# Encoder kernel: x and memory also laid out by features, first feed-forward group by blocks of features, x added afterwards

## The chip, the core and the metric

The kernel runs on one core of a Trainium2 chip. The core has TensorE (PE in the profile: matmuls, and PEld: weight loads), VectorE (DVE), ScalarE (ACT), GpSimd (POOL) and SyncE (SP), and 16 DMA engines that all of them start transfers on. SP and ACT start plain transfers; POOL starts those that add to what lies at the destination. The metric is the time of one execution on the device in microseconds, as the median of several runs.

## The reference

Two layers of an encoder over 512 tokens of 1,024 features, all in float32:

```python
for i in range(DEPTH):                     # DEPTH = 2
    y = swiglu(x, ffn_w_gate[i, 0], ffn_w_up[i, 0], ffn_w_down[i, 0])
    x = layer_norm(ALPHA * x + 0.5 * y, ln_g[i, 0], ln_b[i, 0])
    y = mixer_ab(...) if i % 2 == 0 else mixer_c(...)
    x = layer_norm(ALPHA * x + y, ln_g[i, 1], ln_b[i, 1])
    y = memory_attn(x, mem, mem_w_q[i], mem_w_kv[i], mem_w_o[i])
    x = layer_norm(ALPHA * x + y, ln_g[i, 2], ln_b[i, 2])
    y = swiglu(x, ffn_w_gate[i, 1], ffn_w_up[i, 1], ffn_w_down[i, 1])
    x = layer_norm(ALPHA * x + 0.5 * y, ln_g[i, 3], ln_b[i, 3])

def swiglu(x, w_gate, w_up, w_down):       # d_ff = 2816
    return (jax.nn.silu(x @ w_gate) * (x @ w_up)) @ w_down
```

`memory_attn` attends from 512 tokens to 256 memory tokens, whose keys and values are projections of `mem` (256 x 1,024). The mixers attend among the 512 tokens.

## The kernel before

**Numbers in two parts.** Every float32 operand of a product is split into a high part (a cast to float32r on ACT) and a remainder (a subtraction on DVE): `split` at L296. A product is then three matmuls, high x high, high x remainder, remainder x high: `mm3` at L307.

**Where things lie.** The residual x stands in four tiles of 128 tokens x 1,024 features (`self.x`). For products that contract over features, x also stands transposed in `self.xh` and `self.xl` (128 features x 8 blocks x 512 tokens). `to_features` (L384) makes them: four 128x128 transposes on PE into a PSUM bank, then a split out of it.

**A feed-forward step** (`ffn`, L608) goes over five groups of 2 x 256 hidden columns and a rest. For each group it computes the hidden activations of the two column blocks c1 and c2 (`hidden`, L502: 96 matmuls of 512 columns each), then `down_fast` (L518) multiplies them with the down weights by seven block products (Strassen-Winograd), whose sums of weights come partly from accumulating DMAs of POOL, partly from DVE mixes. Its products m are added to halves of the x tiles by DVE when they leave PSUM (`into`, L574); products 1 and 6 go to a separate tile u2. Product 1 of the first group is written by ACT instead (L590). `rest` runs products 7 and 4.

**The opening.** For the first group's c1 (`ffn_by_tokens`, L473), the tokens are the stationary side: for each of four token blocks 2 x 8 x 3 matmuls of 256 columns, so the first block can start once 128 tokens are there. In the very first step (`first`) it also loads x (`load_x`, L1230: 128 rows of 4 KB per tile, in the order of the grid's columns), transposes it, and loads the first weights in between. The gated activations are turned round at the end by eight transposes.

**Memory** (`memory_tokens`, L1137) is called once inside each mixer: it loads `mem` by tokens, transposes it in 16 pieces on PE and splits it.

**Tiles and order.** Tiles come from pools with a fixed number of buffers: 27 "slab" (4 KB per partition), 2 "raw" (8 KB, landing place of weights), 14 "t2" (2 KB), and PSUM banks 3 "a", 2 "d", 3 "t". Operations are recorded in program order (`Graph.record`, L131) and emitted (`emit`, L168) in the order that a list scheduler works out from guessed costs; every engine and DMA queue then runs its own list in order. Buffers of a pool are granted first come, first served in program order. `nc.after` adds an ordering for that planner alone: with it `masks` (two constant tiles) is placed behind the last DMA recorded so far. Because all operations are recorded by helpers, they all carry the line L143 in the profile, and tiles tell them apart: "a", "d" and "t" are PSUM banks (or the t2 tiles, which also show as "t"), "ident" is the identity matrix of the transposes.

Of the kernel before, what the change touches and what calls it, by code (L numbers as in the profile page):

```python
# [24 lines left out]
KB = D // P  # L25
DFF = 2816
MEM = 256
GRID_W = 64
ROWS = S // GRID_W
# [223 lines left out]
class Kernel:  # L253
# [56 lines left out]
        mm(ps, st[0], mv[1], start=False, stop=False, **kw)  # L310
        mm(ps, st[1], mv[0], start=False, stop=last, **kw)

    def weights(self, srcs, shape, pieces, between=None):

        nc = self.nc
        raw = self.tile(self.raw, [P, *shape], F32, "raw")
        for part, src in srcs:
            nc.sync.dma_start(out=part(raw), in_=src)
            if between:
                between()  # L320
                between = None
        got = []
        for piece in pieces:
            v = piece(raw)
            shp = list(v.shape)
            wh, wl = self.slab(F32R, shp), self.slab(F32R, shp)
            self.split(v, wh, wl)
            got.append((wh, wl))
        return got
# [5 lines left out]
            [(lambda r: r, src)], (KB, 256), [lambda r, i=i: r[:, :, i * P : (i + 1) * P] for i in range(2)]  # L335
        )

    def w_cols_k(self, w, c0, between=None):

        src = w[:, c0 : c0 + 256].rearrange("(k p) f -> p k f", p=P)  # L340
        half = [lambda r, i=i: r[:, 4 * i : 4 * i + 4, :] for i in range(2)]
        return self.weights([(half[i], half[i](src)) for i in range(2)], (KB, 256), half, between)

    def w_cols512(self, w, c0):

# [124 lines left out]
            nc.vector.tensor_tensor(out=dst, in0=halves(pu), in1=halves(sg), op=ALU.mult)  # L470
        return sg

    def ffn_by_tokens(self, wg, wu, first, dst):  # L473

        between = None
        if first:
            self.load_x(0, 0, 512)
            self.to_features(0, [0])
            self.nc.after = self.nc.ops[-1], {"scalar", "vector"}
            between = lambda: (self.load_x(0, 512, D), self.to_features(0, [1]))  # L480
        gate, up = self.w_cols_k(wg, 0, between), self.w_cols_k(wu, 0)
        if first:
            self.nc.after = None
            for t in range(1, NT):
                self.load_x(t)
        sgs = []
        for t in range(NT):
            if first and t > 0:
                self.to_features(t)
            both = []  # L490
            for w, tag in ((gate, "a"), (up, "d")):
                ps = self.ps(tag)
                for k in range(KB):
                    mv = [z[:, k % 4, :] for z in w[k // 4]]
                    self.mm3(ps[:, :256], self.xT(k, t * P, (t + 1) * P), mv, k == 0, k == KB - 1)
                both.append(ps[:, :256])
            sgs.append(self.gated(*both, 256))
        for b in range(2):
            ps = self.transposed([(t * P, P, sgs[t][:, b * P : (b + 1) * P]) for t in range(NT)])
            self.nc.scalar.copy(dst[:, :, b, :], ps.rearrange("p (s n) -> p s n", s=2))  # L500
# [14 lines left out]
        self.split(z, hi, lo, scale)  # L515
        return hi, lo

    def down_fast(self, h1, h2, w, r1, r2, coef, u2, last):  # L518

# [3 lines left out]
        nc = self.nc  # L523
# [54 lines left out]
        banks = {}  # L578

        def run(*steps, blocks=range(2)):  # L580
            for m, tag in steps:
                for b in blocks:
                    ps = banks[m, b] = self.ps(tag) if isinstance(tag, str) else banks[tag, b]
                    for q in range(2):
                        st = [z[:, q * 256 + b * P : q * 256 + (b + 1) * P] for z in left[m]]
                        self.mm3(
                            ps, st, [z[:, q] for z in right[m]], isinstance(tag, str) and q == 0, q == 1, skip_group_check=True
                        )
                    v = into[m](b)
                    if m == 1 and first:  # L590
                        nc.scalar.activation(v, ps, AF.Copy, scale=coef)
                    else:
                        c = -coef if m in (5, 7, 3) else coef
                        nc.vector.scalar_tensor_tensor(out=v, in0=ps, scalar=c, in1=v, op0=ALU.mult, op1=ALU.add)

        def gather(*places):
            for t, n in places if last else ():
                op = ALU.add if n is n1 else ALU.subtract
                nc.gpsimd.tensor_tensor(out=x[t][:, n], in0=x[t][:, n], in1=u2[:, t % 2], op=op)

        run((1, "d"), (6, "t"))
        gather((0, n2), (1, n2), (2, n1), (3, n1))
        run((2, 1), (5, "t"))
        gather((2, n2), (3, n2))
        run((3, 5))
        return u2, lambda *blocks: run((7, "d"), (4, 7), blocks=blocks)

    def ffn(self, i, ln_i, last, aside=None):  # L608

        nc = self.nc  # L610
        wg, wu, wd = (self.a[n][i] for n in ("ffn_w_gate", "ffn_w_up", "ffn_w_down"))
        coef, u2 = 0.5 / ALPHA, None
        for g, (c1, c2) in enumerate(((0, 1024), (256, 1280), (512, 1536), (768, 1792), (2048, 2304))):
            h1, h2 = (self.slab(F32, (P, 2, 2, 256)) for _ in range(2))
            if g == 0:
                self.ffn_by_tokens(wg, wu, i == 0, h1)
            else:
                self.hidden(wg, wu, c1, h1)
            self.hidden(wg, wu, c2, h2)
            u2, rest = self.down_fast(h1, h2, wd, c1, c2, coef, u2, g == 4)  # L620
            if g < 4:
                rest(0, 1)
            if g == 0 and aside:
                nc.after = [op for op in nc.ops if op.dma][-1], {"sync"}
                aside()
# [510 lines left out]

    def memory_tokens(self):  # L1137

        raw = self.tile(self.raw, [P, 2, D], F32, "raw")
        self.nc.sync.dma_start(out=raw, in_=self.a["mem"].rearrange("(m p) d -> p m d", p=P))  # L1140
        self.mt = []
        for kk in range(4):
            ps = self.transposed(
                [(j * 256 + m * P, P, raw[:, m, (2 * kk + j) * P : (2 * kk + j + 1) * P]) for j in range(2) for m in range(2)]
            )
            self.mt.append(self.split_t2(ps))

    def memory(self, i, ln_i, last):
        nc, a = self.nc, self.a
# [77 lines left out]
        gb = self.load_ln(ln_i)  # L1227
        self.down(acts[4:], self.w_rows(w_o, 512) + self.w_rows(w_o, 768), 1.0 / ALPHA, {"gb": gb, "last": last})

    def load_x(self, t, lo=0, hi=D):  # L1230
        src = self.a["x"].rearrange("(r c) d -> c r d", c=GRID_W)[16 * t : 16 * t + 16, :, lo:hi]
        self.nc.sync.dma_start(out=self.x[t][:, lo:hi], in_=src)

    def masks(self):
        self.band = self.tile(self.cst, [P, 384], F32, "band")
# [63 lines left out]
def _layout(inputs):  # L1299
    v = {k: np.ascontiguousarray(np.asarray(z)) for k, z in inputs.items()}  # L1300
    rpb = np.pad(v["c_rpb"][0], ((0, 0), (0, 0), (BIAS_L, BIAS_R)))
    a = {
        "x": v["x"].reshape(S, D),
        "mem": v["mem"].reshape(MEM, D),
        "ln_g": v["ln_g"].reshape(8, D),
        "ln_b": v["ln_b"].reshape(8, D),
        "ffn_w_gate": v["ffn_w_gate"].reshape(4, D, DFF),
        "ffn_w_up": v["ffn_w_up"].reshape(4, D, DFF),
        "ffn_w_down": v["ffn_w_down"].reshape(4, DFF, D),
        "ab_w_in": v["ab_w_in"][0],  # L1310
        "ab_w_out": v["ab_w_out"][0],
        "ab_q_gain": v["ab_q_gain"],
        "ab_k_gain": v["ab_k_gain"],
        "ab_sink": v["ab_sink"],
        "c_w_in": v["c_w_in"][0],
        "c_w_out": v["c_w_out"][0],
        "rpb_g": np.stack([rpb[:, 7 - i : 15 - i, :].transpose(0, 2, 1) for i in range(ROWS)], axis=1),
        "mem_w_q": v["mem_w_q"],
        "mem_w_kv": v["mem_w_kv"],
        "mem_w_o": v["mem_w_o"],  # L1320
    }
    a.update(_constants())
    return {k: np.ascontiguousarray(z) for k, z in a.items()}
# [14 lines left out]
```

## Time and profile before

| | us |
|---|---|
| median of 3 runs | 2215.97 (2215.14 to 2216.75) |
| span of the profiled execution, first to last instruction | 2218.7 |
| PE busy in it | 2185.8 |
| DVE busy | 1415.7 |
| ACT busy | 878.2 |
| POOL busy | 318.0 |

Of the profiled execution only the span is known. It is about 0.1% above the median of the runs.

The profile is of one execution. A timeline row reads: start, duration, engine, line, operation, output tile <- input tiles, shape, count, and in brackets the idle time of the engine before it and what ended that. A row of a table of stretches reads: the stretch and its length, then for PE, PEld, DVE, ACT and POOL the busy time and (x) the instructions, then the granted TensorE clock, the busy share of the DMA engines and the GB/s that they moved. A row of the chain in order of time reads: start, duration, what the chain ran through. A matmul row's duration includes the time in the pipeline, so the pace of matmuls is read from the distance of their starts.

### The profile page before, as it was taken

Reading aid. Unit: us, or ns where it says so; the run is one execution under the profiler, and the core shown is the slowest. Engines: PE = TensorE matmul, PEld = TensorE weight load, DVE = VectorE, ACT = ScalarE, POOL = GpSimd, SP = SyncE. Lnnn points to the kernel's source line nnn. Section 1 sums busy time; section 2 is a strip of 40 time slices with the busy share of each in tenths; the row PEclk is TensorE's granted clock in tenths of the full one; section 3 lists DMA queues with packets and bytes.
Section 4 is the critical chain, followed back from the end, with each engine's and each line's share of the span. In section 5 each row is a group of like instructions: output and inputs, shape, how many; then the busy total and the mean of one; then the engine's idle time right before and its main releaser. Section 6 shows DMA issues by size and latency. Waiting matters only on the chain.

```text
span 2218.7 us, 28479 instructions
## 1 busy us (share of the span) xinstructions
PE 2185.8 (99%) x11264; PEld 1863.8 (84%) x11264; DVE 1415.7 (64%) x2127; ACT 878.2 (40%) x1412; POOL 318.0 (14%) x431
## 2 busy tenths in 40 slices
PE   8999999999999999999999999999999999999998
PEld 7888888778998988888888888888989989888886
DVE  5566657788745756655765566567767557566556
ACT  4333333466443433333333233245554434333331
POOL 0000022544000000000300001214330000000002
PEclk9999999999999999999999999999999999999999
DMA  7443333102442642334334444235553325433342
GB/s 222 143 142 120 106 107 104 39 10 70 130 133 96 182 135 95 95 121 149 120 105 131 143 142 147 95 102 148 141 157 124 124 96 161 124 100 93 111 152 67
DMA packets 195221, 265.15 MB, mean 120 GB/s; under 512 B 8848, under 2 KB 139536, under 8 KB 195088
## 3 DMA queue, kind: packets, MB, share of 16 engines
q1 hardware_dynamic: 181136, 231.88, 32.9%
q0 software_dynamic: 13952, 31.46, 6.6%
q8 instruction: 88, 1.44, 0.3%
q14 instruction: 45, 0.37, 0.1%
HBM read 248.63 MB, written 4.19 MB: 114 GB/s over the span
## 4 chain that ended last, share of the span: by engine, by line
PE 94%; DVE 3%; ACT 1%; POOL 1%; DMA 1%; issue 1%; SPq 0%; DVEq 0%; POOLq 0%; ACTq 0%
PE a L143 59%; PE d L143 21%; PE t L143 14%; DVE slab L143 1%; DVE t L143 1%; ACT slab L143 1%; DVE x L143 0%; POOL slab L143 0%; DMA raw<-ab_w_out 0%; ACT t L143 0%; DMA slab<-t 0%; POOL rms8y L143 0%; ACT junk L143 0%; DMA x<-x 0%; POOL lny L143 0%
## 5 line engine op out<-in xcount | busy, mean ns | idle before, releaser
L143 PE MATMUL a<-xh,slab 128*128 128x512 f32 (+1 forms) x2960 | 892.9, 382 | 0.0
L143 PEld LDWEIGHTS a<-xh,slab 128*128 128x128 f32 x2960 | 549.1, 188 | 106.8
L143 PE MATMUL a<-xl,slab 128*128 128x512 f32 (+1 forms) x1480 | 565.1, 382 | 0.0
L143 PE MATMUL d<-slab,slab 128*128 128x512 f32 (+2 forms) x1856 | 448.8, 381 | 3.3 <-ACT slab L143 3.3
L143 DVE TENSOR_TENSOR slab<-raw,slab 128x1024 fp32r<-128x1024 f32 x300 | 368.8, 1250 | 92.7 <-ACT slab L143 92.2
L143 PEld LDWEIGHTS d<-slab,slab 128*128 128x128 f32 x1856 | 334.5, 188 | 67.3 <-ACT slab L143 5.1
L143 ACT CAST slab<-raw 128x1024 fp32r<-128x1024 f32 x300 | 304.3, 1048 | 206.2 <-DMA raw<-ffn_w_gate 176.4
L143 DVE TENSOR_TENSOR slab<-slab,slab 128x1024 fp32r<-128x1024 f32 (+2 forms) x220 | 254.0, 1177 | 177.8 <-ACT slab L143 104.7
L143 PEld LDWEIGHTS a<-xl,slab 128*128 128x128 f32 x1480 | 278.3, 188 | 53.4
L143 PE MATMUL a<-slab,slab 128*128 128x256 f32 (+3 forms) x1720 | 301.2, 321 | 3.7 <-DMA slab<-t 1.4
L143 PEld LDWEIGHTS a<-slab,slab 128*128 128x128 f32 x1720 | 250.0, 190 | 31.4 <-DVE slab L143 4.6
L143 ACT ACTIVATE t<-a 128x512 f32<-128x512 f32 (+3 forms) x105 | 58.1, 554 | 525.7 <-PE a L143 525.6
L143 ACT CAST slab<-slab 128x1024 fp32r<-128x1024 f32 (+1 forms) x180 | 174.3, 1000 | 135.6 <-DVE slab L143 135.5
L143 POOL DMA_DIRECT2D slab<-ffn_w_down x40 | 48.6, 1255 | 1008.7 <-DMA slab<-ffn_w_down 639.6
L143 PE MATMUL t<-slab,slab 128*128 128x512 f32 (+1 forms) x792 | 185.4, 380 | 0.0
L143 PEld LDWEIGHTS t<-slab,slab 128*128 128x128 f32 x792 | 142.9, 188 | 29.8
L143 DVE TENSOR_TENSOR slab<-a,t 128x512 f32<-128x512 f32 x72 | 49.8, 692 | 175.7 <-PE a L143 175.7
L143 DVE TENSOR_TENSOR slab<-t,slab 128x512 fp32r<-128x512 f32 (+2 forms) x213 | 133.1, 649 | 40.0 <-ACT slab L143 39.5
L143 ACT CAST slab<-t 128x512 fp32r<-128x512 f32 (+2 forms) x213 | 114.6, 565 | 100.9 <-PE t L143 61.8
L143 DVE SCALAR_TENSOR_TENSOR x<-d,x 128x512 f32<-128x512 f32 x168 | 114.9, 686 | 47.4 <-PE d L143 46.9
L143 POOL TENSOR_TENSOR t<-t,l 128x256 f32<-128x256 f32 (+2 forms) x104 | 84.2, 831 | 344.1 <-DVE l L143 343.8
L143 PE MATMUL a<-slab,xh 128*128 128x256 f32 (+1 forms) x432 | 101.2, 328 | 2.2 <-ACT slab L143 1.6
(104 smaller groups left out, 1912.5 us busy)
## 6 DMA issues: line engine op xcount, KB each, us to landing
slab<-ffn_w_down SPq DMA_DIRECT2D x100, 512.0 KB
raw<-ffn_w_gate SPq DMA_DIRECT2D x40, 1024.0 KB
raw<-ffn_w_up SPq DMA_DIRECT2D x40, 1024.0 KB
slab<-ffn_w_down POOLq DMA_DIRECT2D x40, 512.0 KB, 9.7
slab<-t SPq DMA_DIRECT2D x96, 128.0 KB
raw<-mem_w_kv SPq DMA_DIRECT2D x8, 1024.0 KB
raw<-mem_w_kv SPq DMA_DIRECT2D x16, 512.0 KB
raw<-mem_w_q SPq DMA_DIRECT2D x8, 1024.0 KB
```

The costliest lines, as they stand in the source:

```text
L143: op.call = lambda: fn(*args, **kw)
```

## The change

The host also passes `x_t` (features x tokens, the tokens in the grid's column order) and `mem_t` (features x memory tokens). The first group of the first feed-forward step computes its c1 by blocks of features (`ffn_by_features`): after a memset and eight matmuls on zeros (`warm`), it loads x and the gate and up weights in five steps of 1, 1, 2, 2 and 2 feature blocks, splits them, and adds each block's products to four PSUM banks, with the weights as the stationary side and 512 tokens as columns. The first step's two weight loads are issued by ACT, all others by SP. The x tiles are no longer loaded at the start: in the first group the products that would be added to them are written by ACT (`fresh`), and after the group x is added to the four tiles by accumulating DMAs of POOL (`add_x`). Memory is loaded by features and split from where it lands.

```diff
+    def warm(self, n):
+
+        nc = self.nc
+        zero = self.junk[:, :512]
+        nc.vector.memset(zero, 0.0)
+        ps = self.ps("t")
+        for i in range(n):
+            nc.tensor.matmul(ps, zero[:, :P], zero, start=i == 0, stop=i == n - 1)
+
+    def ffn_by_features(self, wg, wu, dst):
+
+        nc = self.nc
+        self.warm(8)
+        steps = [(0, 1), (1, 2), (2, 4), (4, 6), (6, 8)]
+        xT = self.a["x_t"].rearrange("(k p) n -> p k n", p=P)
+        raws = [[self.slab(F32, (P, 4, 256)) for _ in range(2)] for _ in range(2)]
+        got = [[[self.slab(F32R, (P, 4, 256)) for _ in range(2)] for _ in range(2)] for _ in range(2)]
+        banks = [[self.ps(tag) for _ in range(2)] for tag in "ad"]
+        for lo, hi in steps:
+            xs = self.slab(F32, (P, 2, 512))
+            n = hi - lo
+            nc.sync.dma_start(out=xs[:, :n], in_=xT[:, lo:hi, :])
+            q, at = lo // 4, slice(lo % 4, lo % 4 + n)
+            for raw, w in zip(raws, (wg, wu)):
+                src = w[:, 0:256].rearrange("(k p) f -> p k f", p=P)
+                (nc.sync if lo else nc.scalar).dma_start(out=raw[q][:, at, :], in_=src[:, lo:hi, :])
+            self.split(xs[:, :n], self.xh[:, lo:hi, :], self.xl[:, lo:hi, :])
+            for raw, parts in zip(raws, got):
+                self.split(raw[q][:, at, :], parts[q][0][:, at, :], parts[q][1][:, at, :])
+            for k in range(lo, hi):
+                for parts, pair in zip(got, banks):
+                    for b, ps in enumerate(pair):
+                        st = [z[:, k % 4, b * P : (b + 1) * P] for z in parts[k // 4]]
+                        self.mm3(ps, st, self.xT(k, 0, S), k == 0, k == KB - 1)
+        for b in range(2):
+            self.gated(banks[0][b], banks[1][b], dst=dst[:, :, b, :])
...
-    def down_fast(self, h1, h2, w, r1, r2, coef, u2, last):
+    def down_fast(self, h1, h2, w, r1, r2, coef, u2, last, fresh=False):
...
-                    if m == 1 and first:
-                        nc.scalar.activation(v, ps, AF.Copy, scale=coef)
+                    c = -coef if m in (5, 7, 3) else coef
+                    if m == 1 and first or m in (2, 5, 3, 4) and fresh:
+                        nc.scalar.activation(v, ps, AF.Copy, scale=c)
                     else:
-                        c = -coef if m in (5, 7, 3) else coef
                         nc.vector.scalar_tensor_tensor(out=v, in0=ps, scalar=c, in1=v, op0=ALU.mult, op1=ALU.add)
...
-            if g == 0:
-                self.ffn_by_tokens(wg, wu, i == 0, h1)
+            if g == 0 and i == 0:
+                self.ffn_by_features(wg, wu, h1)
+            elif g == 0:
+                self.ffn_by_tokens(wg, wu, h1)
             else:
                 self.hidden(wg, wu, c1, h1)
             self.hidden(wg, wu, c2, h2)
-            u2, rest = self.down_fast(h1, h2, wd, c1, c2, coef, u2, g == 4)
+            u2, rest = self.down_fast(h1, h2, wd, c1, c2, coef, u2, g == 4, i == 0 and g == 0)
             if g < 4:
                 rest(0, 1)
+            if g == 0 and i == 0:
+                for t in range(NT):
+                    self.add_x(t)
...
-        raw = self.tile(self.raw, [P, 2, D], F32, "raw")
-        self.nc.sync.dma_start(out=raw, in_=self.a["mem"].rearrange("(m p) d -> p m d", p=P))
+        raw = self.tile(self.raw, [P, KB, MEM], F32, "raw")
+        self.nc.sync.dma_start(out=raw, in_=self.a["mem_t"].rearrange("(k p) m -> p k m", p=P))
         self.mt = []
         for kk in range(4):
-            ps = self.transposed(
-                [(j * 256 + m * P, P, raw[:, m, (2 * kk + j) * P : (2 * kk + j + 1) * P]) for j in range(2) for m in range(2)]
-            )
-            self.mt.append(self.split_t2(ps))
+            self.mt.append(self.split_pair(raw[:, 2 * kk : 2 * kk + 2, :].rearrange("p k m -> p (k m)")))
...
-    def load_x(self, t, lo=0, hi=D):
-        src = self.a["x"].rearrange("(r c) d -> c r d", c=GRID_W)[16 * t : 16 * t + 16, :, lo:hi]
-        self.nc.sync.dma_start(out=self.x[t][:, lo:hi], in_=src)
+    def add_x(self, t):
+        src = self.a["x"].rearrange("(r c) d -> c r d", c=GRID_W)[16 * t : 16 * t + 16]
+        self.nc.gpsimd.dma_start(out=self.x[t], in_=src, accum_op=ALU.add)
...
-        "mem": v["mem"].reshape(MEM, D),
+        "x_t": v["x"].reshape(ROWS, GRID_W, D).transpose(2, 1, 0).reshape(D, S),
+        "mem_t": v["mem"].reshape(MEM, D).T,
```

More of the change, by code (lines that the diff above doesn't have):

```diff
@@ L311, in mm3, with weights @@
         mm(ps, st[1], mv[0], start=False, stop=last, **kw)
-    def weights(self, srcs, shape, pieces, between=None):
+    def weights(self, srcs, shape, pieces):
         nc = self.nc
@@ L318, in weights @@
             nc.sync.dma_start(out=part(raw), in_=src)
-            if between:
-                between()
-                between = None
         got = []
@@ L336, in w_cols, with w_cols_k @@
         )
-    def w_cols_k(self, w, c0, between=None):
+    def w_cols_k(self, w, c0):
         src = w[:, c0 : c0 + 256].rearrange("(k p) f -> p k f", p=P)
         half = [lambda r, i=i: r[:, 4 * i : 4 * i + 4, :] for i in range(2)]
-        return self.weights([(half[i], half[i](src)) for i in range(2)], (KB, 256), half, between)
+        return self.weights([(half[i], half[i](src)) for i in range(2)], (KB, 256), half)
     def w_cols512(self, w, c0):
@@ L471, in gated @@
         return sg
[L473 to L485, printed above, removed]
+    def warm(self, n):
[5 more added lines that the diff above has]
+            nc.tensor.matmul(ps, zero[:, :P], zero, start=i == 0, stop=i == n - 1)
@@ L486, in ffn_by_tokens @@
+    def ffn_by_tokens(self, wg, wu, dst):
+        gate, up = self.w_cols_k(wg, 0), self.w_cols_k(wu, 0)
         sgs = []
         for t in range(NT):
-            if first and t > 0:
-                self.to_features(t)
             both = []
```

## The prediction, made before the changed kernel had run

> **What bounds the kernel now.** The page comes first: how busy each engine is, and the chain of waits that ends last.
>
> ```profile
> span 2218.7 us, 28479 instructions
> PE 2185.8 (99%) x11264; PEld 1863.8 (84%) x11264; DVE 1415.7 (64%) x2127; ACT 878.2 (40%) x1412; POOL 318.0 (14%) x431
> PE 94%; DVE 3%; ACT 1%; POOL 1%; DMA 1%; issue 1%; SPq 0%; DVEq 0%; POOLq 0%; ACTq 0%
> ```
>
> TensorE (PE) holds 94% of the chain. So time falls only where PE does less, runs faster or waits less, and the next view is busy time by stretch of 50 us, which shows where PE is not full.
>
> ```profile
> 0.00:50.00 50.00, 42.76 (x280) 39.13 (x281) 25.90 (x30) 25.23 (x34) 3.38 (x9) 1.00 0.87 247
> 100.00:150.00 50.00, 50.00 (x222) 41.27 (x221) 31.44 (x40) 16.45 (x21) 0.05 (x1) 1.00 0.23 76
> 500.00:550.00 50.00, 48.26 (x289) 41.35 (x288) 41.57 (x129) 34.26 (x95) 24.77 (x53) 1.00 0.23 63
> 1650.00:1700.00 50.00, 48.83 (x265) 41.77 (x264) 41.56 (x64) 23.23 (x35) 4.36 (x10) 1.00 0.37 126
> ```
>
> The first number after the stretch's length is PE's busy time. The first feed-forward layer is full (50.00) but for its opening, where 7.24 us are idle; the mixers, where memory is prepared, lack 1 to 2 us. The chain in order of time says what the opening waits for, and the timeline gives PE's pace there.
>
> ```profile
> 0.72 3.52 DMA x<-x
> 4.38 1.10 PE t L143 x4
> 9.14 0.95 ACT slab L143
> 10.11 1.24 DVE slab L143
> 8.34 0.58 PE L143 MATMUL a<-slab,xh 128*128 128x256 f32 x1
> 10.00 0.41 PE L143 MATMUL a<-slab,xl 128*128 128x256 f32 x1
> 10.64 0.41 PE L143 MATMUL a<-slab,xl 128*128 128x256 f32 x1
> 12.78 0.28 PE L143 MATMUL a<-slab,xl 128*128 128x256 f32 x1
> 13.14 0.28 PE L143 MATMUL a<-slab,xl 128*128 128x256 f32 x1
> 38.77 0.48 PE L143 MATMUL a<-xh,slab 128*128 128x512 f32 x1
> 39.47 21.58 PE a L143 x95
> ```
>
> Three products of 256 columns take 0.64 us at 10 us (0.21 each) and 0.36 us at 13 us (0.12 each): until about 12 us PE runs at half pace. Between, it waits for the casts (ACT) and remainders (DVE) of whole half-weights. The first half-group ends where the products of `hidden(c2)` take over for good. The last eight transposes are mixed with that start: the 21.58 us run starts at 39.47, one 0.23 us product had been done before, so I set the takeover at 39.24 us. That is the mark against which the new opening is measured.
>
> **The new opening, part by part.** By tokens PE did 192 products of 256 columns and 32 + 8 transposes; by features it does 96 products of 512 and no transpose. The pace of both:
>
> ```profile
> 43.43 0.39 PE L143 MATMUL a<-xl,slab 128*128 128x512 f32 x1
> 44.11 0.39 PE L143 MATMUL a<-xl,slab 128*128 128x512 f32 x1
> 24.95 1.14 PE L143 MATMUL t<-ident,x 128*128 128x128 f32 x9
> ```
>
> Three 512-column products take 44.11 - 43.43 = 0.68 us, 0.227 each, so 96 take 21.8 us (192 x 0.12 = 23.0 before). Transposes are pitched at about 0.11 us ((1.14 - 0.27)/8, with 0.27 for a single one: 1.10/4 at the start), so the 40 removed were 4.4 us.
>
> When can the first product start? It needs one 128-feature block of x (256 KB) and of the gate weight (128 KB).
>
> ```profile
> 0.72 1.28 ACT L143 ACT_TABLE_LOAD   x1 [0.72 <-PEq L1331]
> 1.47 0.57 SPq L143 DMA_DIRECT2D raw<-ffn_w_gate  x1
> 8.55 0.59 ACT L143 CAST xh<-t 128x512 fp32r<-128x512 f32 x1 [1.52 <-PE t L143]
> 531.03 0.37 ACT L143 CAST slab<-t 128x256 fp32r<-128x256 f32 x1 [1.81 <-PE t L143]
> 9.17 0.69 DVE L143 TENSOR_TENSOR xl<-t,xh 128x512 fp32r<-128x512 f32 x1 [0.88 <-ACT xh L143]
> ```
>
> The first x transfer, of the same 256 KB, landed at 0.72 + 3.52 = 4.24 us. Early end: both there at 4.24, cast of x 0.59, cast of the weight 0.37: 5.2 us. Late end: the two new weight DMAs stand on ACT's queue behind its table load, so from 2.0 us; landed 3.52 us later, at 5.5; a second x block's cast slips in front (0.59), then 0.37: 6.5 us. I take 5.7, nearer the early end, because the transfer is small and the order of ACT's queue is unknown. Behind those two issues (0.57 us each) wait only casts that lack data.
>
> Clock: eight products of zeros, 512 columns each, at the half pace seen above take 8 x 0.43 = 3.4 us, from about 1 us (a memset on an idle DVE goes first) to 4.5. In that time PE has nothing else, so they delay nothing. If they open the full clock by themselves the loss is 0. If they do nothing, PE needs about 3.9 us of unbroken products, as from 8.34 to 12.2 here, and loses half of it, 1.95. They stop about 1.2 us before data come, and gaps do close the clock again:
>
> ```profile
> 1460.00:1470.00 10.00, 9.22 (x56) 9.25 (x57) 7.59 (x11) 2.17 (x5) 0.46 (x1) 0.67 0.11 28
> ```
>
> After waits of 1 to 2 us in the second layer the granted clock (third number from the end) is 0.67 for this stretch. I take 1.2, between the two.
>
> Feeding: SP's queue gets 13 DMAs instead of 9, each about 0.6 us, in order of use. 4.2 MB must land (2 MB x, 2 MB weights), as before.
>
> ```profile
> 8.00:10.00 2.00, 2.00 (x10) 1.77 (x9) 0.98 (x2) 1.45 (x3) 0.00 (x0) 1.00 1.09 348
> 16.00:18.00 2.00, 1.91 (x16) 1.91 (x17) 0.34 (x2) 0.00 (x0) 0.00 (x0) 1.00 1.00 205
> ```
>
> The last column is GB/s. At some 320, all is there 13 us after 2.2, at 15.3; the last block pair is due at 5.7 + 1.2 + 6 x 2.73 = 23.3, so PE sets the pace. At 205, which is what the strided token rows of x gave (the new x is one contiguous block per step), it lands at 22.7 and its splits take 2 us: 1.4 us of stall. I take 0.3. ACT and DVE split 1,024 columns per block, about 0.95 and 1.24 us by the chain's rows, under PE's 12 x 0.227 = 2.73. The weights of `hidden(c2)` no longer wait for a raw buffer, and would be there by 22 us.
>
> The opening ends at 5.7 + 21.8 + 1.2 + 0.3 = 29.0 us instead of 39.24: **10.2 us saved** (ends: 12.2, with 5.2 and no loss; about 6, with 6.5, 1.95, 1.4 and another 1.5 for waits inside the first blocks).
>
> Fresh evictions: eight writes of x go from DVE to ACT; DVE was the fuller of the two, PE covers both: nothing. `masks` loses its early place on SP (its order now follows the last `add_x`); its tiles are read hundreds of us later: nothing.
>
> **x added later.** Four 512 KB accumulating DMAs are issued on POOL's queue after group 0's last evictions, near 80 us on the old clock. POOL waits there for these evictions; behind it stand only the two accumulating weight loads of group 1. Who waits for those:
>
> ```profile
> slab<-ffn_w_down POOLq DMA_DIRECT2D x40, 512.0 KB, 9.7
> 87.06 1.19 POOL L143 DMA_DIRECT2D slab<-ffn_w_down  x1
> 95.59 1.23 DVE L143 TENSOR_TENSOR slab<-slab,slab 128x1024 f32<-128x1024 f32 x1 [3.78 <-DMA slab<-ffn_w_down]
> 102.00 0.69 DVE L143 TENSOR_TENSOR slab<-a,t 128x512 f32<-128x512 f32 x1 [2.65 <-PE a L143]
> 112.88 0.69 DVE L143 TENSOR_TENSOR slab<-a,t 128x512 f32<-128x512 f32 x1 [3.61 <-PE a L143]
> 100.00:105.00 5.00, 5.00 (x24) 4.14 (x23) 3.00 (x4) 1.57 (x2) 0.00 (x0) 1.00 0.01 4
> ```
>
> The mix at 95.59 (t1 + b22) already waits 3.78 us for such a load, and DVE works in order: its later `gated` at 102.00 frees the "a" bank in which the last quarter of the hidden products begins, at about 112.8 (the next `gated`, at 112.88, ends the quarter before). From the mix to the end of that `gated` DVE needs some 4.5 us (1.23, 1.3 until a cast, 1.23, 0.69), so it would be through at 100.1 + D, where D is how much later the load lands, and PE stalls only for D above 12.7. The 2 MB are strided token rows; at the 205 GB/s these had in the opening they cost 10.2 us of DMA time, if all of it goes ahead of the loads. After 100 us the DMA engines are idle (4 GB/s), so it goes no further. Price taken: 0; ends 0 and, with the four one after another at 9.7 us each (D = 39), 26.
>
> The first use of x itself, group 1's second eviction, comes 40 us later: covered.
>
> **Memory tokens.** Per mixer, 16 transposes go; the split reads the loaded tile.
>
> ```profile
> 523.63 0.38 SPq L143 DMA_DIRECT2D raw<-mem  x1
> 549.20 1.47 PE L143 MATMUL t<-ident,raw 128*128 128x128 f32 x12
> 1647.33 1.47 PE L143 MATMUL t<-ident,raw 128*128 128x128 f32 x12
> 1652.72 0.66 PE L143 MATMUL t<-ident,raw 128*128 128x128 f32 x4 [1.17 <-DVE slab L143]
> ```
>
> 32 x 0.11 = 3.5 us of PE, and one wait of 1.17 for a bank that they filled themselves. They may partly fill gaps that stay (the mixers' stretches above are not full): 0. At best 4.7. Four casts and four remainders per mixer stay and can now come earlier in the queues, in front of softmax work: 0.69 for each remainder, 2.8 us lost at the worst if one mixer's four all delay the chain. I take 3.2 saved. The load's rows shrink from 4 KB to 1 KB, as those of the weights; it starts some 25 us before it is used in the first mixer: nothing.
>
> Sum: 10.2 + 3.2 = 13.4 us. Only the span of the profiled execution is known, 2218.7; that becomes 2205.3. The median of the runs, 2215.97, lies 2.7 below that span; less 13.4 it is **2202.6 us**.
>
> **A rule of the skill.** The Trainium skill (TensorE: Matmul & The Clock Gate, Part 1) says that the full clock comes only after a busy window of about 3.4 us, counted in windows that run freely. By this, zeros of 3.4 us that are followed by a gap rarely fill one, and the result is the first rival. The trace's 3.9 us of half pace agrees with the window's length; nothing here shows where the windows lie.
>
> **Rivals.**
> 1. The zeros open nothing. Half pace then lasts 3.9 us from 5.7, or up to twice that where waits inside the first blocks break it, so 1.95 to 3.9 are lost in place of 1.2: 2203.4 to 2205.3, middle 2204. For it: the gap before data; against it: PE would be busy for most of 1 to 9 us.
> 2. The transposes of memory only filled gaps: 2202.6 + 3.2 = 2205.8. For it: the gaps of the mixers; against: PE has no idle time ahead of the rows at 549.20 and 1647.33.
> 3. DMA feeds the opening at 205 GB/s and the first product comes at 6.5: end at 6.5 + 21.8 + 1.2 + 1.4 + 1.5 = 32.4, 6.8 saved in place of 10.2: 2206.
> 4. Slower: the accumulating DMAs run one after another, and hold up group 1's accumulated loads on POOL's queue. With D = 39 PE stalls 39 - 12.7 = 26.3 us; 2202.6 + 26.3 = 2229. It decides from D = 12.7 and turns the sign at D = 26. For it: DVE already waits there; against: the 9.7 us are from issue to landing beside other traffic, two at a time.
> 5. Its gain is lost elsewhere, since the order of all engines is planned from guessed times and a shifted start can reorder the mixers: 2216.
>
> **How the numbers follow.** Forecast 0.60, first rival 0.15, second 0.10, third 0.06, fourth 0.06 (half of it above D = 26 and slower, a sixth of it no change, the rest still faster), fifth 0.03. A measurement of this kernel tells 0.2%, 4.4 us, from no change. Faster: 0.60 + 0.15 + 0.10 + 0.06 + 0.02 = 0.93; same 0.04; slower 0.03. The best ends of all terms (12.2 + 4.7) give 2199.1; with half a microsecond of drift, 2198.5 is the low end. The high end holds rivals 1 to 3 and the worst opening (6) without memory's gain, 2210.
>
> **What would show it.** In the changed profile: no transposes of x in the opening; zeros from about 1 us; the first real product at 5.2 to 6.5; three 512-column products in 0.68 us from about 8 us; `hidden(c2)` beginning at 27 to 32; no transposes from the memory tile; the mix of group 1 waiting up to 10 us longer on DVE, with PE still at 50.00 in 50 to 100 and 100 to 150. It is wrong if PE shows idle time near 100 us, if the start comes after 33 us, or if the mixers' idle time grows by what the transposes took.

## The result, and the profile after

| | before | after |
|---|---|---|
| median of the runs, us | 2216.22 (2215.14 to 2216.75) | 2206.13 (2205.21 to 2206.59) |
| span of the profiled execution, us | 2218.7 | 2204.8 |

Both medians are of four runs; the three of the kernel before that were known at the time of the prediction are among its four. The ratio on record is 0.9949, with an interval of 0.9937 to 0.9962: 11.3 us faster (8.4 to 14.0). The two medians alone differ by 10.1 us, which lies inside that interval. The page of the changed kernel opens with:

```profile
span 2204.8 us, 28191 instructions
PE 2176.9 (99%) x11104; PEld 1848.0 (84%) x11104; DVE 1410.4 (64%) x2121; ACT 882.1 (40%) x1419; POOL 321.1 (15%) x435
```

The same stretches as before, with the one after the opening added (columns: stretch, length, then busy time and instructions of PE, PEld, DVE, ACT and POOL, granted clock, DMA share, GB/s):

```profile
0.00:50.00 50.00, 46.94 (x194) 35.72 (x195) 28.00 (x34) 24.46 (x33) 3.33 (x9) 1.00 0.79 242
50.00:100.00 50.00, 49.95 (x221) 40.95 (x220) 26.78 (x31) 23.18 (x31) 5.76 (x6) 1.00 0.75 205
100.00:150.00 50.00, 50.00 (x222) 41.23 (x221) 31.52 (x39) 16.13 (x20) 2.41 (x2) 1.00 0.43 131
500.00:550.00 50.00, 48.48 (x291) 42.17 (x290) 43.89 (x123) 34.49 (x91) 21.34 (x40) 1.00 0.33 85
1650.00:1700.00 50.00, 49.98 (x315) 45.09 (x314) 40.93 (x57) 23.22 (x33) 4.60 (x8) 1.00 0.36 111
...
359.99:743.44 383.45, 372.46 (x2122) 320.37 (x2121) 275.96 (x558) 194.71 (x402) 106.78 (x154) 1.00 0.28 86
1446.91:1846.21 399.30, 395.92 (x2472) 355.51 (x2472) 264.53 (x490) 190.98 (x386) 81.14 (x145) 1.00 0.46 135
...
1450.00:1455.00 5.00, 3.64 (x18) 3.39 (x18) 4.03 (x7) 2.40 (x5) 1.61 (x3) 0.66 0.17 52
```

PE's idle time in the first 50 us fell from 7.24 to 3.06 us, PE stays full to 150 us, and the second layer's mixer is full too (49.98), but the first layer's at 500 us is as empty as before. These rows compare equal times; equal work lies some 9 us earlier after the change, or more, so the long rows below decide. The two long rows are cut at step marks, the starts of the steps' last layer norms: each holds a mixer and the memory step behind it. The same two of the kernel before:

```profile
368.93:752.41 383.48, 373.91 (x2138) 321.91 (x2137) 275.02 (x558) 194.74 (x401) 106.25 (x154) 1.00 0.28 86
1455.75:1860.20 404.45, 398.73 (x2488) 358.34 (x2488) 265.12 (x490) 190.86 (x386) 81.17 (x145) 0.99 0.45 133
...
1460.00:1465.00 5.00, 4.22 (x20) 4.25 (x21) 4.44 (x8) 1.79 (x3) 0.46 (x1) 0.50 0.20 52
1465.00:1470.00 5.00, 5.00 (x38) 5.00 (x37) 3.15 (x4) 0.38 (x2) 0.00 (x0) 0.85 0.02 3
```

So the 13.9 us between the two spans lie in two places: the first step ends 368.93 - 359.99 = 8.94 earlier, and the second mixer with its memory step is 404.45 - 399.30 = 5.15 shorter (the rest became 0.2 longer). The first mixer with its memory step, whose 16 transposes were put at 1.8 us, gives 383.48 - 383.45 = 0.03.

The last rows show what has to be taken off before the 5.15 is read. Around waits of 1.1 to 1.4 us PE runs for a while at half pace: before, 5 x (1 - 0.50) + 5 x (1 - 0.85) = 3.25 us were lost there (3.40 with the row ahead of them, at 0.97), after, 5 x (1 - 0.66) = 1.7.

The opening in the timeline of the changed kernel:

```profile
1.18 3.46 PE L143 MATMUL t<-junk 128*128 128x512 bf16 x8 [1.18 <-DVE junk L143]
5.91 0.50 PE L143 MATMUL a<-xh,slab 128*128 128x512 f32 x1 [1.27 <-ACT slab L143]
6.25 0.40 PE L143 MATMUL a<-xl,slab 128*128 128x512 f32 x1
...
6.71 0.40 PE L143 MATMUL a<-xl,slab 128*128 128x512 f32 x1
...
26.45 1.28 ACT L143 ACTIVATE t<-a 128x512 f32<-128x512 f32 x2 [7.95 <-PE a L143]
27.62 1.98 ACT L143 CAST slab<-raw 128x1024 fp32r<-128x1024 f32 x2
28.06 0.39 PE L143 MATMUL d<-xh,slab 128*128 128x512 f32 x1
28.71 0.50 PE L143 MATMUL a<-xh,slab 128*128 128x512 f32 x1 [0.27 <-ACT slab L143]
...
29.66 0.51 PE L143 MATMUL a<-xh,slab 128*128 128x512 f32 x1 [0.21 <-ACT slab L143]
30.02 2.00 ACT L143 CAST slab<-raw 128x1024 fp32r<-128x1024 f32 x2
...
92.64 1.23 DVE L143 TENSOR_TENSOR slab<-slab,slab 128x1024 f32<-128x1024 f32 x1 [10.04 <-DMA slab<-ffn_w_down]
```

Zeros run from 1.18 to 4.64, the first real product comes at 5.91, and two products take 0.46 us (6.25 to 6.71, with one at 6.48 between), which is full pace at once. c1's last product starts at 28.06. Then comes a loss that the prediction does not have: the first products of `hidden(c2)` come one by one (28.71, 29.66), each waiting for ACT, which is still casting c2's weights (27.62, 30.02). The chain of waits shows where PE takes over for good:

```profile
30.43 21.17 PE a L143 x92
```

Of 96 products 92 are in this run, so the mark corresponds to 30.43 - 4 x 0.227 = 29.52, against 39.24 before and 29.0 forecast. In the four other profiles that start at full pace it is 29.0 to 29.2.

### The profile page after: what moved, and what is told of

It reads as the page before. It is cut to its first block, busy times and chain, and to the rows that moved or that the text cites. A ratio compares the mean times of both kernels' runs of the same rounds, so it can differ in the third digit from the quotient of the medians.

```text
span 2204.8 us, 28191 instructions
## 1 busy us (share of the span) xinstructions
PE 2176.9 (99%) x11104; PEld 1848.0 (84%) x11104; DVE 1410.4 (64%) x2121; ACT 882.1 (40%) x1419; POOL 321.1 (15%) x435
## 4 chain that ended last, share of the span: by engine, by line
PE 93%; DVE 3%; ACT 1%; POOL 1%; DMA 1%; issue 1%; SPq 0%; DVEq 0%; POOLq 0%; ACTq 0%
PE a L143 59%; PE d L143 21%; PE t L143 14%; DVE slab L143 1%; DVE t L143 1%; ACT slab L143 1%; DVE x L143 0%; DMA raw<-ab_w_out 0%; ACT t L143 0%; POOL slab L143 0%; DMA slab<-x_t 0%; SPq L143 0%; POOL rms8y L143 0%; DMA slab<-t 0%; ACT junk L143 0%
## 5 line engine op out<-in xcount | busy, mean ns | idle before, releaser
L143 PE MATMUL a<-xh,slab 128*128 128x512 f32 (+2 forms) x2992 | 905.0, 382 | 1.9 <-ACT slab L143 1.7
L143 PEld LDWEIGHTS a<-xh,slab 128*128 128x128 f32 x2992 | 555.0, 188 | 112.5 <-ACT slab L143 3.4
L143 PE MATMUL a<-xl,slab 128*128 128x512 f32 (+2 forms) x1496 | 571.4, 382 | 0.0
L143 DVE TENSOR_TENSOR slab<-raw,slab 128x1024 fp32r<-128x1024 f32 (+1 forms) x304 | 370.3, 1239 | 90.7 <-ACT slab L143 90.2
L143 ACT CAST slab<-raw 128x1024 fp32r<-128x1024 f32 (+1 forms) x304 | 304.3, 1037 | 194.2 <-DMA raw<-ffn_w_gate 165.4
L143 DVE TENSOR_TENSOR slab<-slab,slab 128x1024 fp32r<-128x1024 f32 (+3 forms) x230 | 258.9, 1148 | 184.1 <-ACT slab L143 104.6
L143 ACT CAST slab<-slab 128x1024 fp32r<-128x1024 f32 (+2 forms) x190 | 179.2, 975 | 142.3 <-DVE slab L143 141.7
L143 DVE TENSOR_TENSOR slab<-t,slab 128x512 fp32r<-128x512 f32 (+2 forms) x205 | 127.9, 647 | 38.1 <-ACT slab L143 37.8
L143 PE MATMUL a<-slab,xh 128*128 128x256 f32 (+1 forms) x368 | 85.7, 327 | 0.2 <-ACT xh L143 0.2
```

What stands on the lines that cost most here:

```text
L143: op.call = lambda: fn(*args, **kw)
```

## Experiments

Medians and ratios are against runs of the kernel before on the same chip. Its medians there were 2218.23 (first four below), 2216.86 (next four) and 2217.39 us (last four). A ratio on record can differ by 0.0005 from the quotient of two medians.

| kernel | median, us | ratio (interval) |
|---|---|---|
| before, again | 2218.15 | 0.9999 (0.9990 to 1.0008) |
| opening only | 2209.43 | 0.9960 (0.9946 to 0.9973) |
| memory only | 2214.22 | 0.9982 (0.9973 to 0.9991) |
| no zeros | 2207.47 | 0.9954 (0.9942 to 0.9967) |
| after, again | 2206.09 | 0.9949 (0.9936 to 0.9961) |
| one product of zeros | 2207.84 | 0.9958 (0.9945 to 0.9970) |
| c1's and c2's casts earlier | 2207.40 | 0.9956 (0.9943 to 0.9968) |
| x added three times | 2221.74 | 1.0024 (1.0015 to 1.0034) |
| c2's casts earlier | 2204.12 | 0.9937 (0.9923 to 0.9950) |
| x not added | 2205.30 | 0.9943 (0.9931 to 0.9956) |
| first mixer's memory as before | 2205.81 | 0.9946 (0.9933 to 0.9958) |
| x added twice | 2222.05 | 1.0018 (1.0009 to 1.0027) |

Differences of 1 or 2 us lie inside these intervals, so the verdicts below go by step marks and by rows of the profiles.

**Which part brings what.** The kernel before once more; the change with memory laid out as before; the kernel before with the new memory alone. Of the second's edit:

```diff
-        raw = self.tile(self.raw, [P, KB, MEM], F32, "raw")
...
+        raw = self.tile(self.raw, [P, 2, D], F32, "raw")
...
+            ps = self.transposed(
```

> The kernel before, once more, for a second profile and the noise. The first profile of it spans 2218.7 us, but the runs differ by 10.1 us and the two profiles by 13.9. Theory: the first profile was a slow draw, by the half-pace stretch near 1460 us (granted clock 0.67); this one spans 2214 to 2216 us with less of it, the ratio is 1.000. Rival: the profile adds some 4 us to this kernel and not to the changed one; then this spans 2218 to 2219 again.

> The changed kernel with memory loaded by tokens and transposed, as before. Theory: the opening brings 9 us, 2207 to 2208 (ratio 0.996). Rival: the opening and the memory part disturb each other's planned order, and this brings all 10 us or only 6.

> The kernel before with memory alone loaded by features. Theory as predicted: 3.2 us less, 2213 us, from 32 transposes of 0.11 us on the path that sets the end. Rival (the transposes filled gaps of the mixers): no difference, 2216, and the marks of the four steps show the time given back within the next step, as the first mixer's 1.2 us were in the memory step.

The opening alone gains 2218.23 - 2209.43 = 8.8 us, memory alone 4.0 (2.0 to 6.0 by its interval), so the medians can't tell the 3.2 us of the theory from 2 or 5; the product of the two ratios is 0.9942, within the interval of the whole change: the parts add. Memory alone by the step windows:

```profile
369.28:751.49 382.21, 371.44 (x2122) 318.95 (x2121) 275.97 (x558) 194.50 (x401) 106.73 (x154) 1.00 0.27 87
1455.13:1854.50 399.37, 395.74 (x2472) 355.39 (x2472) 264.09 (x490) 190.92 (x387) 81.27 (x145) 1.00 0.45 135
```

Read plainly, the first mixer gained 383.48 - 382.21 = 1.27. But the kernel before had one stretch at half pace there that cost 1.70, and this execution had none. The table gives both steps less such losses (the sum of 1 - granted clock times length, over rows of 5 us):

| profile | memory by | first, us | half pace | rest | second, us | half pace | rest |
|---|---|---|---|---|---|---|---|
| before | tokens | 383.48 | 1.70 | 381.78 | 404.45 | 3.40 | 401.05 |
| before, again | tokens | 383.46 | 1.70 | 381.76 | 402.94 | 3.45 | 399.49 |
| memory only | features | 382.21 | 0 | 382.21 | 399.37 | 1.70 | 397.67 |
| after | features | 383.45 | 1.70 | 381.75 | 399.30 | 1.70 | 397.60 |
| after, again | features | 382.19 | 0 | 382.19 | 397.58 | 0 | 397.58 |

The first mixer gains nothing, the second some 2.7 us (400.3 with a third profile by tokens, that of the opening alone, 400.39; against 397.6). The three by tokens lie between 399.5 and 401.1, so the 2.7 could be 1.9 to 3.4. It also leaves something open: in the second mixer all three profiles by tokens lost 3.4 at half pace, and of eleven by features one lost 3.45, the others 1.7 or nothing. Whether the new memory changes this or it is chance isn't shown; by the medians of memory alone, 4.0, both are possible. To see the first by itself in the changed kernel, its memory alone was put back:

```diff
-                self.memory_tokens()
+                self.memory_by_tokens()
```

> The changed kernel with memory loaded by tokens and transposed in the first mixer, by features in the second. Theory (the first mixer's transposes filled gaps, the second's were on the path): without the half-pace stretches the time is that of the changed kernel within 0.5 us; PE's idle time of the first mixer is 1.2 us less than in the changed kernel (11.0) and the step as long. Rival: 1.8 us longer.

```profile
361.58:743.58 382.00, 372.42 (x2138) 320.80 (x2137) 274.95 (x558) 194.53 (x401) 106.08 (x154) 1.00 0.27 87
1447.05:1844.65 397.60, 394.47 (x2473) 354.01 (x2472) 263.85 (x490) 190.84 (x387) 80.88 (x145) 1.00 0.45 136
```

Neither stretch lost anything to half pace here. With the transposes PE is busy 372.42 us and the step takes 382.00; without them, in the second profile of the change, it is busy 371.12 and takes 382.19. The 16 transposes filled time in which PE waits anyway. The rows show where, first without them, then with them:

```profile
540.68 1.42 PE L143 MATMUL d<-slab,slab 128*128 128x512 f32 x5 [0.97 <-DVE x L143]
553.61 3.01 PE L143 MATMUL d<-slab,slab 128*128 128x512 f32 x12 [0.59 <-DVE slab L143]
...
540.54 1.47 PE L143 MATMUL t<-ident,raw 128*128 128x128 f32 x12
552.64 1.78 PE L143 MATMUL d<-slab,slab 128*128 128x256 f32 x8 [0.16 <-ACT slab L143]
```

Without the transposes PE waits 0.97 + 0.59 us for results of DVE; with them only 0.16. The second mixer keeps its gain, as it kept the new memory.

**What the zeros do.** No zeros, one product of them, and the change again:

```diff
-        self.warm(8)
+        self.warm(1)
```

> The changed kernel without the memset and the eight products of zeros. Theory (the zeros open the full clock): the first products go at 0.43 us instead of 0.23 for 3.4 to 4 us from 5.9, and the time is 1.7 to 2 us longer, 2208 us. Rival (products start late enough for the clock, or DMA sets the pace there anyway): half pace shows, but the time stays within 0.7 us.

> The changed kernel with one product of zeros instead of eight; every engine's order is the same otherwise (leaving out all eight had moved the banks and with them the order of the later steps, which hid 2 us). Theory: half pace for the first 3.4 to 6 us of real products, the first step is 2.1 us longer than in the changed kernel, and the time is 2.1 longer. Rival: DMA and casts set the pace of these first blocks, so less than 1 us is lost.

> The changed kernel again, as the reference for the runs beside it. From the profiles so far: what is left after taking away the half-pace stretches of the two mixers (1.7 us each, none to three of them in a profile) is 8.9 us for the opening, 0 for memory in the first mixer and 2.6 in the second. Theory: the ratio to before is 0.9947 (11.6 us), the profile shows the same steps when its half-pace stretches are taken away. Rival (memory's part is the predicted 3.2, evenly): the first mixer with the memory step is 1.6 us shorter than in the kernel before.

Without any zeros one "t" bank is not taken at the start, and steps far behind it changed (the two feed-forward steps between 744 and 1449 us took 2 us longer), so the run with one product is the cleaner one:

```profile
1.18 0.61 PE L143 MATMUL t<-junk 128*128 128x512 bf16 x1 [1.18 <-DVE junk L143]
5.84 0.79 PE L143 MATMUL a<-xh,slab 128*128 128x512 f32 x1 [4.06 <-ACT slab L143]
6.43 0.63 PE L143 MATMUL a<-xl,slab 128*128 128x512 f32 x1
6.86 0.63 PE L143 MATMUL a<-xh,slab 128*128 128x512 f32 x1
...
10.53 0.39 PE L143 MATMUL d<-xh,slab 128*128 128x512 f32 x1
10.75 0.39 PE L143 MATMUL a<-xh,slab 128*128 128x512 f32 x1
```

The first real product is not delayed or brought forward (5.84), but products stand 0.43 us apart until about 10.4 and 0.22 after, and the first step ends at 361.35 instead of 359.99 and 359.34. So the zeros are worth 1.4 to 2.0 us where they work. They don't always: with the same eight zeros and first product, the run with the first mixer's memory put back has

```profile
6.03 0.79 PE L143 MATMUL a<-xh,slab 128*128 128x512 f32 x1 [1.25 <-ACT slab L143]
6.62 0.63 PE L143 MATMUL a<-xl,slab 128*128 128x512 f32 x1
7.04 0.63 PE L143 MATMUL a<-xh,slab 128*128 128x512 f32 x1
```

that is, half pace, and its first step ends at 361.58, so that this opening gains 368.93 - 361.58 = 7.4 us. Of nine profiles with eight products of zeros, five start at full pace and four at half. In three of the five the zeros took 3.43 to 3.49 us, in all others 3.59 or 3.60: in those three the pace rose while they still ran.

**What delays c2.** The order of ACT's queue was planned from guessed times, in which every load runs at 205 GB/s; the opening's loads ran at 347 GB/s (16 to 18 us). The planner was therefore told shorter loads, first for all early ones, then for those behind the first weights only:

```diff
-        op.ns = self.cost(engine, method, outs[0], ins, kw)
+        op.ns = self.cost(engine, method, outs[0], ins, kw) * (205 / 340 if engine == "sync" and 52 < op.index < 400 else 1)
```

> The changed kernel with the planner's guess for the first SP transfers at 340 GB/s, as measured, instead of 205: it then puts the four casts of the c2 weights ahead of the first Silu on ACT. Theory (the 1.4 us lost at the start of c2 are PE waiting for casts that stand behind Silu though their data had landed): the c2 run ends 1.4 us earlier and the time is 1 to 1.4 us shorter. Rival (the data had not landed): the same 1.4 us are lost, waiting for DMA.

> The changed kernel with the planner's faster guess for the SP transfers from the third step on only (with it for all of them, ACT cast the second step's weights ahead of the first step's, and the first product came at 7.34 us, at half pace, in place of 5.91). ACT's order is that of the changed kernel up to the first Silu, and has the four c2 casts ahead of it. Theory: first product at 5.9, no wait at the start of c2, the first step 1.2 to 1.4 us shorter than in the changed kernel (its last layer norm starts at 358.2 instead of 359.3 to 360.0), the time shorter by as much. Rival: the down products that follow wait for what is then late, and the first step ends where it did.

The first missed: the planner now put later casts ahead of the first block's, and the first real product slipped from 5.91 to 7.34. c2 did start without a wait. The second has both:

```profile
18.10 2.00 ACT L143 CAST slab<-raw 128x1024 fp32r<-128x1024 f32 x2 [2.39 <-DMA raw<-ffn_w_gate]
21.09 2.00 ACT L143 CAST slab<-raw 128x1024 fp32r<-128x1024 f32 x2 [0.98 <-DMA raw<-ffn_w_up]
27.48 1.28 ACT L143 ACTIVATE t<-a 128x512 f32<-128x512 f32 x2 [2.14 <-PE a L143]
29.10 0.39 PE L143 MATMUL d<-xh,slab 128*128 128x512 f32 x1
29.32 0.39 PE L143 MATMUL a<-xh,slab 128*128 128x512 f32 x1
```

c2's casts run at 18.10 and 21.09, ahead of the Silu at 27.48, and c2's first product follows c1's last (29.10) at once. Its chain has all 96 products in one run:

```profile
29.48 21.76 PE a L143 x96
```

From c1's last product to the end of this run it takes 29.48 + 21.76 - 29.10 = 22.14 us, in the change 30.43 + 21.17 - 28.06 = 23.54, so 1.40 are saved at c2's start. From c1's last product to the end of the step it takes 359.07 - 29.10 = 329.97 us, in the change 359.99 - 28.06 = 331.93: the new order is worth 1.96 in this pair, 1.7 to 2.0 against the other profiles. What the 0.3 to 0.6 beyond the wait are is not shown. This opening began at half pace and the step still ended as early as any, though 0.9 later than expected. It has the lowest median of all kernels here, 2204.12; its interval overlaps the change's, so that it is faster than the change rests on the rows, not on the times.

**What adding x costs.** x not added, added twice, three times (the last one's edit):

```diff
-                for t in range(NT):
-                    self.add_x(t)
+                for n in range(3):
+                    for t in range(NT):
+                        self.add_x(t)
```

> The changed kernel without adding x (the four accumulating DMAs are left out, so x counts as zero there). PE's and DVE's orders are the same. Theory (the added transfers are hidden): the time is the same within 0.5 us of the changed kernel, and the mix of group 1 begins some 6 us earlier, near 86. Rival: the four DMAs cost part of what the opening missed of the forecast, and this is 1 us or more faster.

> The changed kernel with x added twice (2 MB more; the output is that of another x). With x added three times the mix began at 109.6 and PE idled 14.6 us, so its limit there was 95.0, not the 99 us that my forecast gives on this clock. Theory (the limit is set on ACT: a cast of the mixed tile stands ahead of the Silu that frees the bank): the stall is the mix's start less 95.0 us. Rival (the limit is the DVE gate, 99 us): the stall is the start less 99. I expect the mix near 101.

> The changed kernel with x added three times instead of once (12 accumulating DMAs, 4 MB more; the output is that of another x). In the changed kernel the mix that waits for the accumulated load began 6.3 us later than before, of 12.7 that PE can bear. Theory: some 20 us more on POOL's queue, the mix begins about 20 us later, PE idles 13 to 15 us before the last quarter of the hidden products, and the time is longer by that. Rival (the extra bytes fit, since the DMA engines were idle after 100 us, and nobody waits): less than 3 us longer.

The mix of group 1, which waits for the accumulated weights, without the additions:

```profile
83.23 1.23 DVE L143 TENSOR_TENSOR slab<-slab,slab 128x1024 f32<-128x1024 f32 x1 [1.09 <-DMA slab<-ffn_w_down]
```

With them it starts at 92.64 (above), so D = 92.64 - 83.23 = 9.4 us. Of this 0.5 is a later end of c1 in that profile (28.06 against 27.60); the second profile of the change, with c1's last product at 27.55, has the mix at 92.00, which makes D = 8.8. Without the additions I had expected it near 86. The delay costs nothing: the first step ends at 359.27 without the additions and at 359.34 in the second profile of the change. What is late is already the issue of the accumulated load on POOL, first without, then with the additions:

```profile
73.14 1.20 POOL L143 DMA_DIRECT2D slab<-ffn_w_down  x1 [45.14 <-DMA slab<-ffn_w_down]
...
83.63 1.21 POOL L143 DMA_DIRECT2D slab<-ffn_w_down  x1 [10.81 <-issue]
```

POOL stood 10.81 us before it, and the profile names nothing that it waited for. With three times the additions the cover is gone:

```profile
97.51 0.39 PE L143 MATMUL a<-xh,slab 128*128 128x512 f32 x1
109.64 1.23 DVE L143 TENSOR_TENSOR slab<-slab,slab 128x1024 f32<-128x1024 f32 x1 [27.33 <-DMA slab<-ffn_w_down]
110.90 1.04 ACT L143 CAST slab<-slab 128x1024 fp32r<-128x1024 f32 x1 [32.40 <-DVE slab L143]
111.85 0.59 ACT L143 ACTIVATE t<-a 128x512 f32<-128x512 f32 x1
112.50 0.79 PE L143 MATMUL a<-xh,slab 128*128 128x512 f32 x1 [14.60 <-ACT t L143]
```

DVE's mix comes at 109.64; ACT has waited 32.40 us to cast its result (110.90), and only behind that cast in ACT's queue stands the Silu (111.85) that empties the "a" bank; PE stands still for 14.60 us. So PE stalls when the mix starts after 109.64 - 14.60 = 95.0, which is D = 95.0 - 83.2 = 11.8 (11.6 with c1's end, 0.14 later here, taken off). With two additions the same wait appears in PE's list of waits:

```profile
PE a L143 <- ACT t L143: 10.2, 1, 10.2
```

The mix starts at 106.59 there, and 106.59 - 10.2 = 96.4; its opening ran at half pace, its marks some 1.4 later, which makes it 95.0 again, and not 99. The changed kernel has 95.0 - 92.64 = 2.4 us left (2.7 in its first profile and 2.8 in its second, if the limit moves with c1's end). Both kernels end slower than the one before although their stalls, 10.2 and 14.6, are of the size of the gain or little more: PE also runs at half pace after its stall (granted clock 0.52 from 110 to 115 us with two additions, 0.50 from 110 to 115 and 0.70 from 115 to 120 with three). In the profile with two additions PE waits another 2.3 us at 356.65, behind a late small load (`nsink`); the one with three has no such wait. So the time with two additions holds more than the stall, and it is no clean measure of it.

## Why the prediction was right, and where it was not

The time measured, 2206.13, is 0.16% over the 2202.6 forecast, inside the range and with the forecast sign; the likeliest case, x hidden and the opening as the main gain, is the one that happened. Step by step:

- **First product and pace: right.** 5.91 against 5.7, and 5.83 to 6.12 over all profiles but that of the first experiment with the casts. DMA fed the opening at some 347 GB/s, so the third rival (205 GB/s, start at 6.5) is out.
- **Clock: a mean of two cases that both happen.** I took 1.2 us, between 0 and 1.95. The executions give 0 (five of nine) or about 1.4 to 2.0. The first rival ("the zeros open nothing") is true of the other four. The Trainium skill (TensorE: Matmul & The Clock Gate, Part 1) has a window that runs freely and so a cold stretch that varies from run to run, and the traces agree: the same zeros and the same gap of 1.2 to 1.4 us went both ways.
- **End of the opening: near in number, partly by luck.** The takeover by c2 came at 29.52, so 9.7 were saved where 10.2 was forecast (by the step marks 8.9 to 9.6 at full pace, 7.4 at half). Two errors cancel in it: the 1.2 us for the clock were not lost in this execution (c1's last product started at 28.06 and took 0.23, so c1 was done at 28.29), and 29.52 - 28.29 = 1.2 us were lost at c2's start, for which the prediction had nothing. The failed step is "The weights of `hidden(c2)` no longer wait for a raw buffer, and would be there by 22 us". They had landed (casts of them start at 18.10 and 21.09 where the order allows it), but a weight counts from its cast, and ACT's planned order had these casts behind c1's Silu. The experiment that moved them took the 1.4 us at c2's start off, and 1.7 to 2.0 by the end of the step.
- **x added later: right in price and in D** (0; 8.8 to 9.4 against 10.2 at most), **wrong in what sets the limit, and near its number by luck.** I had DVE's order and its `gated` as what frees the bank, and a limit of D = 12.7, which is a mix at 99 us on the new clock; it is ACT's order and its Silu, and a mix at 95.0. That this is D = 11.8, close to 12.7, comes from a mix that without the additions starts at 83.23, some 3 us earlier than I had it. The fourth rival turns the sign earlier than the prediction says: twice the additions (D = 106.59 - 83.23 = 23.4, or 21.8 without the 1.55 us that c1 ends later there) are already slower, not from 26, for the gain was 11 us and not 13.4, and PE also loses its clock.
- **Memory: mis-sized.** 3.2 us for both mixers became 0 in the first and 2.7 in the second. The second rival ("the transposes of memory only filled gaps") is true of the first mixer; the argument against it, no idle time right ahead of the transposes, looked at the wrong place: the idle time that they used comes after them (0.97 us for a result of DVE at 540.68 and 0.59 at 553.61, once they are gone). The second mixer had its 1.8 us of transposes and the wait of 1.17 for their bank on PE's path, 3.0 together, near the 2.7 found (1.9 to 3.4).
- **Order: the fifth rival** didn't come for the whole change; the run without zeros shows that it can, with 2 us.

With the parts as found, 8.9 to 9.6 and 2.7, the gain is 11.6 to 12.3 us at equal clock, against 11.3 by the ratio and 13.9 by the two profiled spans; of that 13.9, 1.7 is the half-pace stretch more that the profile of the kernel before had. These parts are for an opening at full pace, which five of nine profiles had.

What makes DVE's results late in the first mixer, so that PE waits there, was not tried and stays open.

## What to carry to other kernels

When work is moved ahead, price the moment at which its consumer's engine gets round to it, not the moment at which data land: both misses here (c2's start, the limit of D) were an in-order ACT queue in an order planned from guessed loads. Transposes taken off the busiest engine paid here only in the mixer where that engine does not wait later; the busy share right beside them did not tell. Before two profiles are subtracted, take the stretches at half pace out of both, and ask of several profiles whether the change itself makes them rarer.

## What the runs showed of the hardware

- **Half-pace losses came in steps of 1.7 us.** Around a wait of 2.0 us near 390 us and two of 1.4 and 1.1 near 1450, the sums per place were 0, 1.7 or 3.4 to 3.45 in the profiles, and which one changed from one execution of the same kernel to another (1.70 and 1.70 in one of the change, 0 and 0 in the next). The Trainium skill (TensorE: Matmul & The Clock Gate, Part 1) gives a window of 3413 ns; an estimate from it, half a window lost at half pace, is 1.7 us, and the traces agree.
- **The granted clock does not show the opening.** It reads 1.00 from 5 to 8 us in the profiles of the new opening, also where products stand 0.43 us apart. There the pace has to be read from the starts. The row of the run with the first mixer's memory put back:

```profile
5.00:8.00 3.00, 1.97 (x5) 1.59 (x6) 2.47 (x6) 2.17 (x6) 0.00 (x0) 1.00 1.04 362
```

- **Accumulating DMAs put off the accumulated load behind them, not in proportion to their bytes.** The four additions to x, 2 MB, put it off by 8.8 to 9.4 us, 4 MB by 21.8 to 23.4 and 6 MB by 109.64 - 83.23 = 26.4. With 2 MB the load was issued 83.63 - 73.14 = 10.5 us later; what held POOL back is not shown.
